# An encoder trunk on one core: the dense stream of the two merged stages is traced at 0.3 of attention's pace, where it was 1.1

## The chip, the core and the metric

The kernel runs on one core of a Trainium2 chip. The metric is the device time of one execution in microseconds (us), lower is better. Three runs of the kernel before gave 2283.27, 2291.74 and 2292.84 us, median 2291.74 us. The engines are named as the profile names them: PE (matrix multiply; PEld is its weight load), ACT (activations), DVE (vector), POOL (GpSimd) and SP (issues transfers).

## The reference

Two request groups share one set of weights: a prompt of 1024 tokens and a sample of 512, each with 16 learned meta tokens ahead. All is float32. One layer is computed:

```
n = rms_norm(h); qa,ka,va,qb,kb,vb = split(n @ w_in)          # 1024 -> 18 x 128 columns
A: 8 query heads, 2 key/value heads, per-head rms norm, axial rotary, softmax, @ va
B: 4 heads, two softmax maps each: (p0 - lam * p1) @ vb, then rms norm of the head
h = h + concat(A, B) @ w_out
n = rms_norm(h); gate = conv3(n @ w_ff_gate); h = h + (gelu(gate) * (n @ w_ff_up)) @ w_ff_down
y = rms_norm(h)                                                # D_FF = 2816 = 22 x 128
```

## The kernel before

The token axis is the free axis of every dense product. Each weight tile is 128 x 1024 float32 (512 KB). `load_weight` brings it in with a transfer issued from ACT's queue (L146), splits it into a high part (a cast: ACT on L123, or POOL on L150) and a low remainder (DVE, L124 or L151), and `mm3` (L129 to L131) multiplies three times: high by high, high by low, low by high. All weights of the program go through one pool `g.wp`: two raw slots `w_f` and three slots each of `w_hi` and `w_lo`. Slots are handed on in the order in which the tiles were traced, so a tile traced later can't get a slot before one traced earlier.

The program has these stages, all written as Python generators that yield the number of PE columns they have just traced:

1. `projection` of the sample, alone.
2. The first merge: `attention` of the sample with `projection` of the prompt; when attention is done, the rest of the projection is traced at once.
3. The second merge: `attention` of the prompt with the sample's dense stream `f1`, which is `mixer_out` (w_out) and then `conv_glu`: eleven pairs of feature tiles, each pair two gate tiles (chunks of 258 columns), two up tiles (512 columns) and two down tiles (512 columns; the last pair in 256).
4. The third merge: `mixer_out` of the prompt (chunks of 344, 342 and 340 columns, PSUM tag `s`) with what is left of `f1`, at 1.0 to 1.0; then the rest of `f1`, called a drain.
5. `conv_glu` of the prompt, alone. It takes its buffers where the sample's stood.

In attention, `softmax` fills three PSUM banks (`ps_s`, one buffer) with scores (PE, L401 and L402, 348 columns each), takes the row minimum of the negated scores on DVE (L405) and the exponential on ACT (L408). `weighted_v` transposes the probabilities on PE (L422, PSUM `ps_t`, two buffers), splits them (ACT L123, DVE L124, or `pt_hi`, `pt_lo`) and multiplies by v (A: L436, L437; B: L432 to L434; the tail L446) into `ps_o`, which has one buffer. A block of A is one head on 512 queries. The prompt has 16 of them, with a tile of 8 halo queries after each four heads. A differential block of B (L519 to L541) has three column tiles of 114 queries, each with two softmax maps: two exponentials, two scalings on ACT (L524, L527) and an addition on POOL (L528). It ends with a norm that also goes through `ps_o`: ACT copies `ps_o` (L533) and squares it (L535), PE sums (L537), ACT takes Ln, Exp and Square (L112 to L114), DVE two products (L115, L117) and the last product (L540). The prompt has twelve such blocks, after all of A.

What sets the order: `merge` calls whichever of the two generators is behind by its own scale, where `wa` and `wb` are the scales:

```
i = 0 if b is None or done[0] / wa <= done[1] / wb else 1
...
done[i] += next((a, b)[i])
```

It stops when `a` (attention) is done. From the traced order and the slots a scheduler then lays out each engine's instructions, and may put a later-traced instruction ahead of an earlier one where its slots and inputs allow it. At run time each engine runs its list in order.

Of the kernel before, what the change touches and what calls it, by code (L numbers as in the profile page):

```python
# [771 lines left out]
PADD = 8  # L772
ML = 2
NRAW, NW = 2, 3
R1, R2, R3 = (1.0, 1.1), (1.0, 1.1), (1.0, 1.0)


@with_exitstack
# [173 lines left out]
```

## Time and profile before

| what | value |
|---|---|
| median of three runs | 2291.74 us (2283.27 to 2292.84) |
| span of the profiled execution | 2286.9 us |
| median less that span | 4.8 us |
| PE busy | 2136.4 us, 93% of the span |
| DVE busy | 1273.1 us, 56% |
| ACT busy | 1032.2 us, 45% |
| POOL busy | 665.6 us, 29% |
| mean granted PE clock | 0.964 |

A matmul's busy time overlaps with the next one's, so a busy PE may run at very different paces; what a matmul costs in a stream is the distance between two starts. By the trace, the prompt's first scores start at 547.5 us, its last ones end at about 1370 us, its `mixer_out` starts at 1404.55 us and its `conv_glu` at 1524 us.

### The profile page before, as it was taken

Reading aid. Unit: us, or ns where it says so; the run is one execution under the profiler, and the core shown is the slowest. Engines: PE = TensorE matmul, PEld = TensorE weight load, DVE = VectorE, ACT = ScalarE, POOL = GpSimd, SP = SyncE. Lnnn points to the kernel's source line nnn. Section 1 sums busy time; section 2 is a strip of 40 time slices with the busy share of each in tenths; the row PEclk is TensorE's granted clock in tenths of the full one; section 3 lists DMA queues with packets and bytes.
Section 4 is the critical chain, followed back from the end, with each engine's and each line's share of the span. In section 5 each row is a group of like instructions: output and inputs, shape, how many; then the busy total and the mean of one; then the engine's idle time right before and its main releaser. Section 6 shows DMA issues by size and latency. Waiting matters only on the chain.

```text
span 2286.9 us, 32292 instructions
## 1 busy us (share of the span) xinstructions
PE 2136.4 (93%) x12418; PEld 1917.3 (84%) x12418; DVE 1273.1 (56%) x2203; ACT 1032.2 (45%) x1806; POOL 665.6 (29%) x514
## 2 busy tenths in 40 slices
PE   7888989997599999999999987989999999999997
PEld 6887888996488888888999975988888888888887
DVE  6635544455357666766777774774333444433445
ACT  5434544565346434456777785542122211122224
POOL 5862335442023212124444432431110001111004
PEclk9898999997799999999999997999999999999999
DMA  6564645444533332323333313631111111111112
GB/s 209 172 219 88 140 142 137 161 139 141 120 103 67 93 98 76 87 66 100 110 100 102 106 44 120 202 112 56 37 56 47 47 47 46 43 50 56 46 37 75
DMA packets 126739, 222.76 MB, mean 97 GB/s; under 512 B 28888, under 2 KB 79864, under 8 KB 126072
## 3 DMA queue, kind: packets, MB, share of 16 engines
q1 hardware_dynamic: 97784, 115.82, 17.4%
q10 hardware_dynamic: 28800, 104.87, 15.1%
q8 instruction: 98, 1.61, 0.3%
q14 instruction: 57, 0.47, 0.1%
HBM read 172.10 MB, written 48.55 MB: 96 GB/s over the span
## 4 chain that ended last, share of the span: by engine, by line
PE 67%; DMA 4%; DVE 4%; ACT 2%; issue 1%; SPq 0%; POOL 0%; POOLq 0%; DVEq 0%; ACTq 0%
PE ps_mm L129 17%; PE ps_mm L130 17%; PE ps_mm L131 17%; PE ps_t L422 4%; PE ps_s L401 3%; PE ps_s L402 3%; PE ps_o L437 1%; PE ps_o L436 1%; DMA res<-xT 1%; PE ps_o L432 1%; PE ps_o L434 1%; PE ps_o L433 1%; DMA v<-v 1%; DVE w_lo L124 1%; DMA rT<-r_a 1%
## 5 line engine op out<-in xcount | busy, mean ns | idle before, releaser
L129 PE MATMUL ps_mm<-xhi,w_hi 128*128 128x512 f32 (+6 forms) x1968 | 665.2, 338 | 29.5 <-ACT xhi L123 28.5
L130 PE MATMUL ps_mm<-xlo,w_hi 128*128 128x512 f32 (+6 forms) x1968 | 659.3, 335 | 0.0
L131 PE MATMUL ps_mm<-xhi,w_lo 128*128 128x512 f32 (+6 forms) x1968 | 657.4, 334 | 0.0
L129 PEld LDWEIGHTS ps_mm<-xhi,w_hi 128*128 128x128 f32 x1968 | 374.1, 190 | 54.4 <-ACT xhi L123 28.9
L130 PEld LDWEIGHTS ps_mm<-xlo,w_hi 128*128 128x128 f32 x1968 | 373.5, 190 | 25.0 <-issue 0.9
L131 PEld LDWEIGHTS ps_mm<-xhi,w_lo 128*128 128x128 f32 x1968 | 373.2, 190 | 24.1
L123 ACT CAST w_hi<-w_f 128x1024 fp32r<-128x1024 f32 x134 | 139.4, 1048 | 395.7 <-PE ps_mm L130 357.8
L405 DVE TENSOR_SCALAR_CACHE_REDUCE p<-ps_s 114x1044 f32<-114x1044 f32 (+5 forms) x212 | 223.4, 1054 | 130.3 <-PE ps_s L402 121.0
L124 POOL TENSOR_TENSOR a_lo<-gate,a_hi 128x512 fp32r<-128x512 f32 x66 | 100.3, 1520 | 658.1 <-ACT a_hi L123 654.2
L408 ACT ACTIVATE p<-p,nm 114x1040 f32<-114x1040 f32 (+5 forms) x212 | 215.2, 1015 | 89.3 <-DVE p L405 88.6
L123 ACT CAST pt_hi<-ps_t 128x512 fp32r<-128x512 f32 (+6 forms) x360 | 167.0, 484 | 193.1 <-PE ps_t L422 150.0
L699 DVE TENSOR_TENSOR h<-ps_mm,h 128x512 f32<-128x512 f32 (+1 forms) x288 | 182.1, 645 | 123.4 <-PE ps_mm L131 122.6
L124 DVE TENSOR_TENSOR pt_lo<-ps_t,pt_hi 128x512 fp32r<-128x512 f32 (+4 forms) x312 | 170.6, 563 | 118.0 <-ACT pt_hi L123 117.1
L130 PE MATMUL ps_mm<-a_lo,w_hi 128*128 128x512 f32 (+1 forms) x576 | 216.3, 379 | 0.0
L131 PE MATMUL ps_mm<-a_hi,w_lo 128*128 128x512 f32 (+1 forms) x576 | 215.7, 378 | 0.0
L129 PE MATMUL ps_mm<-a_hi,w_hi 128*128 128x512 f32 (+1 forms) x576 | 214.5, 384 | 0.0
L401 PE MATMUL ps_s<-k,q 128*114 128x348 f32 (+4 forms) x552 | 179.5, 331 | 21.5 <-DMA q<-qk 15.1
L422 PE MATMUL ps_t<-ident,p 128*128 128x128 f32 (+7 forms) x1188 | 187.6, 272 | 9.5 <-ACT p L408 6.2
L402 PE MATMUL ps_s<-k,q 128*114 128x348 f32 (+4 forms) x552 | 173.0, 319 | 10.9 <-DMA q<-qk 10.9
L422 PEld LDWEIGHTS ps_t<-ident,p 128*128 128x128 f32 (+7 forms) x1188 | 143.1, 137 | 41.8 <-issue 9.5
L124 DVE TENSOR_TENSOR w_lo<-w_f,w_hi 128x1024 fp32r<-128x1024 f32 x100 | 122.7, 1236 | 81.8 <-ACT w_hi L123 81.7
L687 DVE TENSOR_TENSOR gate<-ps_mm,gate 128x512 f32<-128x512 f32 x66 | 45.6, 691 | 198.3 <-PE ps_mm L131 195.7
(186 smaller groups left out, 3608.3 us busy)
## 6 DMA issues: line engine op xcount, KB each, us to landing
w_f<-w_gate ACTq DMA_DIRECT2D x44, 512.0 KB
w_f<-w_up ACTq DMA_DIRECT2D x44, 512.0 KB
w_f<-w_down ACTq DMA_DIRECT2D x44, 512.0 KB
w_f<-w_in ACTq DMA_DIRECT2D x36, 512.0 KB
w_f<-w_out ACTq DMA_DIRECT2D x32, 512.0 KB
q<-qk SPq DMA_DIRECT2D x48, 256.0 KB
q<-qk SPq DMA_DIRECT2D x48, 171.0 KB
qk<-hi SPq DMA_DIRECT2D x20, 384.0 KB
```

What stands on the lines that cost most here:

```text
L123: nc.scalar.copy(hi, src)
L124: (lo_engine or nc.vector).tensor_tensor(out=lo, in0=src, in1=hi.bitcast(F32), op=ALU.subtract)
L129: nc.tensor.matmul(ps, lhsT=whi, rhs=xhi, start=start, stop=False)
L130: nc.tensor.matmul(ps, lhsT=whi, rhs=xlo, start=False, stop=False)
L131: nc.tensor.matmul(ps, lhsT=wlo, rhs=xhi, start=False, stop=stop)
L401: nc.tensor.matmul(ps[:, i], lhsT=q[0], rhs=kc, start=True, stop=False)
L402: g.mark = nc.tensor.matmul(ps[:, i], lhsT=q[1], rhs=kc, start=False, stop=True).ins
L405: nc.vector.tensor_scalar(out=p.rearrange("p (i w) -> p i w", i=nch), in0=ps, scalar1=-HD ** -0.5, scalar2=3.0e38, op0=ALU.mult, op1=ALU.m ...
L408: nc.scalar.activation(p, p, AF.Exp, bias=nm, scale=-1.0, accum_out=l)
L422: nc.tensor.transpose(tps[:, c:c + M], p[:, k0:k0 + kw], g.ident[:M, :M])
L687: nc.vector.tensor_tensor(out=a, in0=up, in1=a, op=ALU.mult)
L699: nc.vector.tensor_tensor(out=hs, in0=ps, in1=hs, op=ALU.add)
```

## The change

One line of numbers changes. R1 holds the scales of the first merge (attention, then projection), R2 those of the second (attention, then `f1`), R3 those of the third.

```
-R1, R2, R3 = (1.0, 1.1), (1.0, 1.1), (1.0, 1.0)
+R1, R2, R3 = (1.0, 0.3), (1.0, 0.3), (1.0, 1.0)
```

Each instruction stays what it was; only places in the lists change. Up to a point that the run before reached at 615.7 us, PE's list is the same row for row, the whole first merge and the sample's attention included; the lists of ACT, DVE, POOL and SP also first differ in the second merge.

The first place is ACT's list in the second merge, behind the two weight loads of the down tiles that belong to the sample's second feature pair. Before, the next weight is a gate tile of the third pair:

```order
L408 ACTIVATE p,l_a<-p,nm 128x1040
L675 ACT_TABLE_LOAD
L675 ACTIVATE gate<-gate 128x1024
L678 ACT_TABLE_LOAD
L146 DMA w_f<-w_gate 128x1024
L458 COPY o_low<-ps_o 64x8
```

and now it is the first w_out tile of the prompt's `mixer_out`:

```order
L408 ACTIVATE p,l_a<-p,nm 128x1040
L675 ACT_TABLE_LOAD
L675 ACTIVATE gate<-gate 128x1024
L678 ACT_TABLE_LOAD
L146 DMA w_f<-w_out 128x1024
L123 CAST pt_hi<-ps_t 128x512
```

So the prompt's w_out tiles now stand in the weight slots from the end of the second pair on. The loads that follow in this list are one gate, two w_out, one gate and one w_out; then there is no weight load until the prompt's attention has ended.

The second place is PE's list in the eighth of the twelve differential blocks of the prompt, at the end of its product with v. Before, triples of the dense stream (`a_hi`, `a_lo`) stand between the pieces of attention:

```order
L432 MATMUL ps_o<-pt_hi,v 128x342
L433 MATMUL ps_o<-pt_hi,v 128x342
L434 MATMUL ps_o<-pt_lo,v 128x342
L422 MATMUL ps_t<-ident,p 128x114 x3
L129 MATMUL ps_mm<-a_hi,w_hi 128x256
L130 MATMUL ps_mm<-a_lo,w_hi 128x256
L131 MATMUL ps_mm<-a_hi,w_lo 128x256
L446 MATMUL ps_o<-pt_hi,v_tail 128x342
L422 MATMUL ps_t<-ident,p 128x114 x3
L401 MATMUL ps_s<-k,q 114x348
```

and now scores, transposes and products with v follow each other directly:

```order
L401 MATMUL ps_s<-k,q 114x348
L402 MATMUL ps_s<-k,q 114x348
L434 MATMUL ps_o<-pt_lo,v 128x342
L422 MATMUL ps_t<-ident,p 128x114 x3
L446 MATMUL ps_o<-pt_hi,v_tail 128x342
L422 MATMUL ps_t<-ident,p 128x114 x3
L401 MATMUL ps_s<-k,q 114x348
```

This holds from the last dense matmul of the second merge, which now stands ahead of the last 522 of the prompt's 828 score matmuls, to the end of attention.

The third place is PE's list where the sample's `f1` goes from an up tile (`xhi`, `w_lo`) to the down tiles (`a_hi`, `a_lo`) of a pair. Before, this stood in the second merge, and attention's instructions are near:

```order
L131 MATMUL ps_mm<-xhi,w_lo 128x512
L129 MATMUL ps_mm<-a_hi,w_hi 128x512
L130 MATMUL ps_mm<-a_lo,w_hi 128x512
L131 MATMUL ps_mm<-a_hi,w_lo 128x512
L402 MATMUL ps_s<-k,q 128x348
L401 MATMUL ps_s<-k,q 128x348
```

and now, for six of the pairs, it stands behind the prompt's `mixer_out`, with nothing but `f1` itself around it:

```order
L131 MATMUL ps_mm<-xhi,w_lo 128x512
L129 MATMUL ps_mm<-a_hi,w_hi 128x512
L130 MATMUL ps_mm<-a_lo,w_hi 128x512
L131 MATMUL ps_mm<-a_hi,w_lo 128x512
L129 MATMUL ps_mm<-a_hi,w_hi 128x512
L130 MATMUL ps_mm<-a_lo,w_hi 128x512
```

Counted over the lists between PE's first changed row and the prompt's `mixer_out`, the dense matmuls of `f1` before (1200 of 258 columns, 252 of 256, 1008 of 512) become 384, 168 and 192; so 816 of 258, 84 of 256 and 816 of 512 columns now stand behind attention, which is eight and a half of the eleven pairs.

## The prediction

> **What bounds the kernel now.** I first read the busy shares by slice.
>
> ```profile
> PE   7888989997599999999999987989999999999997
> PEclk9898999997799999999999997999999999999999
> ```
>
> PE is nearly full, with two dips: slices 10 and 11 (515 to 629 us, where the second merge begins) and slices 24, 25 and 27 (from 1315 us on, where the prompt's attention ends). Its granted clock is low there too (7 tenths). Then the busy time by stage, cut where PE's list first changes, at the last stretch of attention, at its end, and at the start of the prompt's `conv_glu`:
>
> ```profile
> core 0: us, PE busy (x) PEld busy (x) DVE busy (x) ACT busy (x) POOL busy (x), PEclk, DMA share, GB/s
> 615.70:700.00 84.30, 81.66 (x591) 74.73 (x590) 54.02 (x97) 44.11 (x86) 25.37 (x28) 1.00 0.39 99
> 700.00:1300.00 600.00, 598.91 (x3635) 530.25 (x3635) 429.35 (x714) 362.31 (x600) 191.02 (x155) 1.00 0.33 93
> 1300.00:1404.50 104.50, 87.26 (x516) 75.71 (x514) 68.06 (x126) 77.66 (x137) 31.79 (x23) 0.91 0.22 75
> 1404.50:1524.00 119.50, 106.46 (x600) 101.06 (x601) 87.31 (x131) 66.72 (x123) 55.85 (x47) 0.90 0.54 173
> ```
>
> From 700 to 1300 us PE is busy 598.91 of 600 us, while ACT has 362 and DVE 429: this stage is bound by PE, because dense matmuls fill every wait of attention. What a matmul costs here is the distance of starts (first column):
>
> ```profile
> 881.65 0.28 PE L130 MATMUL ps_mm<-xlo,w_hi 128*128 128x258 f32 x1
> 881.77 0.28 PE L131 MATMUL ps_mm<-xhi,w_lo 128*128 128x258 f32 x1
> ...
> 895.01 0.32 PE L401 MATMUL ps_s<-k,q 128*128 128x348 f32 x1
> 895.17 0.39 PE L437 MATMUL ps_o<-pt_lo,v 128*128 128x512 f32 x1
> 895.40 0.60 PE L422 MATMUL ps_t<-ident,p 128*128 128x128 f32 x4
> 895.75 0.47 PE L129 MATMUL ps_mm<-xhi,w_hi 128*128 128x512 f32 x1
> ...
> 896.30 0.40 PE L131 MATMUL ps_mm<-xhi,w_lo 128*128 128x512 f32 x1
> 896.53 0.39 PE L129 MATMUL ps_mm<-xhi,w_hi 128*128 128x512 f32 x1
> ```
>
> 258 columns cost 0.12 us, scores of 348 cost 0.16, 512 columns 0.23, four transposes 0.35. Dense work thus costs the same wherever it stands, if PE is fed. The question is how full PE is when attention stands alone. The trace shows that near its end, by L537, once per differential block:
>
> ```profile
> 1326.96 0.84 PE L537 MATMUL ps_o<-o_sq,ones_v 128*128 128x342 f32 x2 [0.91 <-ACT o_sq L535]
> ...
> 1351.03 0.74 PE L537 MATMUL ps_o<-o_sq,ones_v 128*128 128x342 f32 x2
> ...
> 1372.10 1.37 PE L537 MATMUL ps_o<-o_sq,ones_v 128*128 128x342 f32 x2
> ...
> 1404.55 0.66 PE L129 MATMUL ps_s<-xhi,w_hi 128*128 128x344 f32 x1 [1.52 <-ACT xhi L123]
> ```
>
> ```profile
> 1351.03:1372.10 21.07, 15.51 (x92) 12.54 (x91) 15.18 (x28) 18.45 (x34) 5.72 (x5) 0.99 0.03 10
> ...
> 557.00:574.70 17.70, 16.02 (x90) 12.78 (x90) 13.53 (x25) 13.38 (x25) 0.00 (x0) 1.00 0.36 82
> ```
>
> Between 1351.03 and 1372.10 no dense matmul runs: one block (its 92 PE instructions) takes **21.07 us with ACT busy 18.45**. By distances of starts the same 92 would need about 12 us: 31 scores and 25 products of 342 columns at 0.16, 33 transposes at 0.09. Alone, the differential block belongs to ACT and its chain, not to PE.
>
> **The change, part by part.** Stage 1 and the first merge cost nothing: no row moves before 615.7 us. There the rest of the projection is traced right behind attention, and the list comes out the same.
>
> In the second merge the stretch from 615.70 to 1404.55 us, 789 us, splits in two.
>
> *With dense work.* Up to the last dense matmul PE now has 228 score matmuls (36 us), 158 products of 512 (37), 336 transposes (30), the halo tile (4), and dense 384 + 168 of about 257 (66) and 192 of 512 (45): 218 us. The stretch 615.70 to 700 held 591 instructions in 84.3 us, or 0.143 each, the PE-full one 0.165; the 1494 rows of this part give 214 to 246 by these. I take **236**: 8% for switching and for a share of attention that is higher than before.
>
> *Attention alone.* Left are 92 products of 512, or 5.4 blocks of A, the second halo tile, and twelve differential blocks. For A:
>
> ```profile
> L405 DVE TENSOR_SCALAR_CACHE_REDUCE p<-ps_s 128x1044 f32<-128x1044 f32 x6 | 7.5, 1244 | 3.6 <-PE ps_s L402 3.5
> L124 DVE TENSOR_TENSOR pt_lo<-ps_t,pt_hi 128x512 fp32r<-128x512 f32 x7 | 4.5, 686 | 0.3 <-ACT pt_hi L123 0.3
> ```
>
> A block has four minima and nine splits: DVE 4 x 1.24 + 9 x 0.69 = 11.2 us, PE 3.8 + 3.2 + 4.0 = 11.0. The stretch 557 to 574.7, with six score tiles and hardly any dense work, took 17.7 us, or 11.8 per four. I take 13 (11 to 15): 70 us, and 5 for the halo. For B, ten periods of 21.1 bring L537 of the tenth block (211), and then 1404.55 - 1372.10 = 32.4 us end the last two, as before. Together **319 us** (A at 11 and B at 18.45, ACT's busy time: 281; A at 15 and B at 24.1, the distance from 1326.96 to 1351.03, which held some 9 us of dense work: 359).
>
> So the prompt's `mixer_out` starts 789 - 236 - 319 = **234 us sooner**.
>
> *What comes later.* Behind it stand 816 + 84 matmuls of about 257 columns at 0.12 and 816 of 512 at 0.234: 107 + 191 = **298 us**, at full pace. Their cover is gone too. From up to down tiles there is a chain:
>
> ```profile
> L687 DVE TENSOR_TENSOR gate<-ps_mm,gate 128x512 f32<-128x512 f32 x22 | 15.1, 688 | 29.0 <-PE ps_mm L131 26.4 <-ACT gate L675 2.5
> ...
> L123 ACT CAST a_hi<-gate 128x512 fp32r<-128x512 f32 x22 | 13.6, 618 | 14.4 <-DVE gate L687 14.3
> ...
> L124 POOL TENSOR_TENSOR a_lo<-gate,a_hi 128x512 fp32r<-128x512 f32 x22 | 32.8, 1489 | 43.1 <-ACT a_hi L123 39.3 <-issue 3.8
> ```
>
> 0.69 + 0.62 + 1.49 = 2.8 us, while the pair's first tile offers six matmuls on two PSUM buffers (1.4 us): some 1.4 us of wait in each of six pairs that stand alone, and a little for evictions into two buffers. I take **+10** (0 to 25).
>
> *The seams.* 1404.5 to 1524 us holds 576 w_out matmuls at 0.16 and little else, about 95 us in 119.5.
>
> ```profile
> 1522.33 1.50 PE L576 MATMUL ps_s<-acc,ones_d 128*128 128x340 f32 x2 [6.56 <-POOL acc L571]
> ```
>
> The 6.56 us at its end are now filled by `f1`; but `f1`'s own last norm and the prompt's eight first norm tiles then stand ahead of `conv_glu`, which I put at 13. Net **+6** (-10 to +15). The queues: ACT's list has no weight load while attention is alone, so no load waits there in front of exponentials; SP's loads of q come for shorter blocks, at a DMA share of 0.33 before.
>
> Sum: -234 + 298 + 10 + 6 = **+80 us**. The span of 2286.9 becomes 2367; the median lies 4.8 above that span, so **2372 us**.
>
> **Two rules.** After a long gap PE's pace falls:
>
> ```profile
> 1377.76 0.65 PE L432 MATMUL ps_o<-pt_hi,v 128*128 128x342 f32 x1 [4.30 <-DVE o_rs L115]
> 1378.21 0.49 PE L433 MATMUL ps_o<-pt_hi,v 128*128 128x342 f32 x1
> 1378.50 0.49 PE L434 MATMUL ps_o<-pt_lo,v 128*128 128x342 f32 x1
> ```
>
> After 4.30 us of waiting the distance is 0.29 us, where 348 columns had 0.16. [...] DVE is also held up by POOL's addition:
>
> ```profile
> 1356.20 2.41 POOL L528 TENSOR_TENSOR p<-p 114x1040 f32<-114x1040 f32 x1 [3.37 <-ACT p L527]
> ...
> 1357.14 1.85 DVE L117 SCALAR_TENSOR_TENSOR o_rs<-o_rs,rs_y 128x342 f32<-128x342 f32 x1
> ...
> 1391.80 0.52 DVE L117 SCALAR_TENSOR_TENSOR o_rs<-o_rs,rs_y 128x342 f32<-128x342 f32 x1
> ```
>
> 1.85 against 0.52 us, on the chain that frees `ps_o`. My 21.07 includes one such hit. [...]
>
> **The rivals.** *The clock falls while attention is alone* (12%). For: both dips of PE carry 7 tenths of clock. Against: 0.99 and 1.00 in the two stretches alone. At 0.29 for 0.16 PE's own work there, some 200 us at full pace (5.4 blocks at 11 and twelve at 12), needs 360 instead of the 319: 2372 + 41 = 2413 us.
>
> *Attention alone is tighter* (12%): blocks at ACT's busy time, no waits in `f1`: part two 281, +10 gone: 2324 us.
>
> *Not slower* (4%). The one mechanism: the differential blocks, freed of dense work, run at PE's 12.1 us instead of ACT's pace. Then ten of them take 121, and the whole comes out at 2372 - 90 = 2282 us. It decides at a period of 13.1 us, where ten blocks have won back the 80. Against it stand 18.45 us of ACT work in every block, which no order makes smaller.
>
> *Nothing moves* (1%): the scheduler could take dense work ahead as it does in the first merge. The lists show that it does not here: the weight slots are taken by w_out tiles, which wait for attention.
>
> **How the numbers follow.** My forecast, 2345 to 2400 us, has 71%. The range reaches to the tight rival's 2324 and beyond the clock's 2413, with waits at 25 and B at 24.1 partly together: 2324 to 2430. What a measurement can tell from no change is 0.5%, 11 us: slower 0.95, as all of the first three cases are (2324 is 1.4% above the median); the last two rivals hold 0.05, 0.03 of it within the 11 us (2282 is) and 0.02 below.
>
> **What would show it.** In the changed profile: PE's slices about 850 to 1170 us fall to 5 to 7 tenths with ACT at 8 or 9; L537 stands 20 to 23 us apart there; `mixer_out` of the prompt starts near 1170 us; `f1` alone follows at over 9 tenths, with waits of 1 to 2 us for `a_lo`; `conv_glu` starts near 1604. I am wrong if L537 is under 17 or over 25 us apart, if dense matmuls still stand there, or if `f1` alone shows waits for weights.

## The result, and the profile after

The changed kernel takes **2448.01 us** (median of four runs, 2446.67 to 2453.54), the kernel before in the same job 2290.18 us (2283.27 to 2292.84): ratio **1.0688**, 95% interval 1.0673 to 1.0703. Slower, as forecast, but by 158 us instead of 80, and above the upper end of the range (2430). The profiled execution has a span of 2446.6 us.

First the page's busy tenths per slice (a slice is now 61 us) in the changed kernel:

```profile
PE   7888999974999998777799999995999999999998
...
PEclk8989999987999998888899999997999999999999
```

The dip that stood at slices 24 to 27 (the end of attention) has become a wide one, slices 16 to 20 (918 to 1223 us), with a clock of 8 tenths, and a new narrow one stands at slice 28 (1651 to 1713 us). Then the windows, cut at the last dense matmul of the second merge, at the first and the tenth differential block (L537), at the prompt's `mixer_out` and at the sample's last norm:

```profile
core 0: us, PE busy (x) PEld busy (x) DVE busy (x) ACT busy (x) POOL busy (x), PEclk, DMA share, GB/s
615.70:859.60 243.90, 240.49 (x1558) 213.00 (x1558) 172.52 (x297) 137.19 (x250) 55.77 (x57) 1.00 0.42 91
859.60:975.90 116.30, 103.38 (x578) 84.31 (x576) 87.14 (x161) 95.00 (x165) 26.74 (x22) 0.94 0.23 61
975.90:1191.60 215.70, 156.59 (x802) 134.26 (x802) 137.90 (x243) 174.72 (x297) 72.76 (x55) 0.86 0.16 54
1191.60:1224.00 32.40, 22.40 (x103) 17.24 (x102) 12.51 (x25) 16.91 (x36) 2.58 (x2) 0.80 0.34 124
1224.00:1662.40 438.40, 407.11 (x2313) 357.42 (x2313) 227.04 (x313) 120.13 (x180) 119.89 (x107) 0.98 0.32 105
1662.40:2446.60 784.20, 754.11 (x3816) 659.71 (x3816) 341.86 (x510) 187.53 (x268) 106.00 (x88) 0.98 0.15 49
```

These rows can be set against the forecast's stretches. The third sum is 119.3 + 298 + 10 + 6, less the 1.5 us of the last norm's own row, at whose start (1522.33 before) both profiles are cut here; from there the kernel before had 2286.9 - 1522.3 = 764.6 us. The 13 us forecast for the seam into `conv_glu` are counted in the third sum, though most of the seam lies behind the cut.

| stretch | forecast | measured | difference |
|---|---|---|---|
| second merge with dense work | 236 | 243.9 | +8 |
| attention alone | 319 | 364.4 | +45 |
| `mixer_out`, rest of `f1` | 432 | 438.4 | +7 |
| from the last norm ahead of the prompt's `conv_glu` to the end | 765 | 784.2 | +20 |

So the plan of the stages was right and two terms were too small: **attention alone** and **the start of the prompt's `conv_glu`**. In the first, nine periods of L537 take 215.7 us, 24.0 each instead of 21.1 (26 of the 45), and A, the halo and the first differential block take 116.3 instead of 96 (20). The last two blocks take 32.4, as forecast.

How such a block looks is told by the timelines of PE, DVE and POOL (start, duration, what, and in brackets the wait ahead of it and its releaser):

```profile
1098.14 0.42 PE L401 MATMUL ps_s<-k,q 128*114 128x348 f32 x1 [1.14 <-DVE p L405]
...
1102.65 0.63 PE L401 MATMUL ps_s<-k,q 128*114 128x348 f32 x1 [3.29 <-DVE p L405]
1103.08 0.49 PE L402 MATMUL ps_s<-k,q 128*114 128x348 f32 x1
1103.37 0.49 PE L401 MATMUL ps_s<-k,q 128*114 128x348 f32 x1
```

```profile
1100.45 0.17 DVE L523 RECIPROCAL r_b<-l_b 114x2 f32<-114x2 f32 x1 [2.36 <-ACT p L408]
1101.34 1.25 DVE L405 TENSOR_SCALAR_CACHE_REDUCE p<-ps_s 114x1044 f32<-114x1044 f32 x1 [0.72 <-POOL p L528]
```

```profile
1098.91 2.39 POOL L528 TENSOR_TENSOR p<-p 114x1040 f32<-114x1040 f32 x1 [3.12 <-ACT p L527]
```

DVE stands at a reciprocal that waits for ACT's exponential, then at a minimum that waits for POOL's addition to end at 1101.30 (it frees a buffer of p). The next scores wait 3.29 us for that minimum, and then PE runs at 0.29 us per 348 columns instead of 0.16. Two suspects suggest themselves, the buffers of p and the lost clock; the experiments speak against both as the main cause. A third, the place of that reciprocal in DVE's list, no run moves by itself.

The second term shows in PE's and DVE's timelines at the seam:

```profile
1662.39 1.22 PE L576 MATMUL ps_mm<-acc,ones_d 128*128 128x256 f32 x2 [8.73 <-POOL acc L571]
1681.31 0.94 PE L129 MATMUL ps_mm<-xhi,w_hi 128*128 128x344 f32 x2 [17.70 <-ACT xhi L123]
```

```profile
1673.01 0.48 DVE L725 SCALAR_TENSOR_TENSOR y<-h,gain,rstd 128x256 f32<-128x256 f32 x1 [1.80 <-DMA yT<-y]
...
1680.81 0.58 DVE L646 SCALAR_TENSOR_TENSOR t<-h,gain,rstd 128x344 f32<-128x344 f32 x1 [3.98 <-DMA yT<-y]
```

PE waits 8.73 and 17.70 us. DVE's products of y (L725) wait for the stores of earlier y tiles, since the sample's y has two buffers, and the prompt's first norm tiles t (L646) stand behind them in DVE's list; one of these waits 3.98 us for a store itself. Before, `f1` ended long ahead of this point and all that was hidden.

### The profile page after: what moved, and what is told of

It reads as the page before. It is cut to its first block, busy times and chain, and to the rows that moved or that the text cites. A ratio compares the mean times of both kernels' runs of the same rounds, so it can differ in the third digit from the quotient of the medians.

```text
span 2446.6 us, 32351 instructions
## 1 busy us (share of the span) xinstructions
PE 2193.2 (90%) x12418; PEld 1940.3 (79%) x12418; DVE 1283.2 (52%) x2203; ACT 1033.8 (42%) x1806; POOL 651.5 (27%) x514
## 5 line engine op out<-in xcount | busy, mean ns | idle before, releaser
L401 PE MATMUL ps_s<-k,q 128*114 128x348 f32 (+4 forms) x552 | 192.0, 353 | 68.3 <-DVE p L405 53.1
L408 ACT ACTIVATE p<-p,nm 114x1040 f32<-114x1040 f32 (+5 forms) x212 | 215.1, 1015 | 52.6 <-DVE p L405 51.9
L402 PE MATMUL ps_s<-k,q 128*114 128x348 f32 (+4 forms) x552 | 180.2, 332 | 12.0 <-DMA q<-qk 12.0
L401 PEld LDWEIGHTS ps_s<-k,q 128*128 128x128 f32 (+3 forms) x552 | 107.1, 194 | 90.5 <-DVE p L405 72.8
L669 ACT ACTIVATE gate<-ps_mm,vec 128x256 f32<-128x256 f32 (+2 forms) x110 | 66.4, 606 | 265.0 <-PE ps_mm L131 249.1
```

The lines of the kernel that those rows point to most:

```text
L401: nc.tensor.matmul(ps[:, i], lhsT=q[0], rhs=kc, start=True, stop=False)
L402: g.mark = nc.tensor.matmul(ps[:, i], lhsT=q[1], rhs=kc, start=False, stop=True).ins
L408: nc.scalar.activation(p, p, AF.Exp, bias=nm, scale=-1.0, accum_out=l)
L669: nc.scalar.activation(a, gp[:, 1:cw + 1], AF.Identity, scale=cw3[1], bias=cb)
```

## The experiments

Each is the changed kernel with one edit, unless another is said. The numbers of a group were taken beside runs of the kernel before on the same chip (median 2282.22 us for e1 to e4, 2280.29 for e5 to e8, 2280.37 for e9 to e12, 2284.26 for e13 and e14), so they are compared by ratio. "Period" is the mean of nine distances of L537 (from the first to the tenth differential block; "fed" where dense matmuls stand between them), "alone" the stretch without dense matmuls that ends at the prompt's `mixer_out` (55 us in the kernel before).

| run | edit | ratio (95%) | alone, us | period, us |
|---|---|---|---|---|
| changed kernel | | 1.0688 (1.0673 to 1.0703) | 364 | 24.0 |
| e1 | rest of `f1` traced first | 0.9881 (0.9856 to 0.9905) | none | fed |
| e2 | ten p buffers | 1.0686 (1.0656 to 1.0716) | 358 | 24.7 |
| e3 | addition on DVE | 1.0675 (1.0648 to 1.0703) | 360 | 23.2 |
| e4 | eight y buffers | 1.0663 (1.0640 to 1.0687) | 364 | 24.0 |
| e5 | own slots for w_out | 1.0379 (1.0360 to 1.0398) | 41 | fed |
| e6 | p in groups | 1.0730 (1.0712 to 1.0747) | 366 | 24.8 |
| e7 | scaling and addition in one | 1.0486 (1.0465 to 1.0507) | 317 | 19.0 |
| e8 | ratio 0.6 | 1.0517 (1.0492 to 1.0541) | 249 | 25.1 |
| e9 | one PSUM buffer | one run, 2605.12 us | 300 | 23.5 |
| e10 | e9 with filling matmuls | one run, 2632.66 us | 325 | 24.7 |
| e11 | e1 with e7 | 0.9889 (0.9870 to 0.9907) | none | fed |
| e12 | e1 at ratio 1.0 | 1.0001 (0.9988 to 1.0014) | 32 | fed |
| e13 | one softmax less per block | one run, 2430.67 us | 357 | 23.5 |
| e14 | second scaling on DVE | one run, 2411.20 us | 344 | 22.7 |

### Is it the slots that keep the dense work out of attention?

e1 moves one line of the trace:

```
             merge(attention(es0, g, 0, "left"), R2[0], f1, R2[1])
         g.psum.relay(s=6)
+        drain(f1)
         st0 = state(ctx, 0, "left", False)
         merge(mixer_out(g, 0, st0, "left", False, "s"), R3[0], f1, R3[1])
```

> The changed kernel with one line moved: the rest of the sample's dense stream is traced right behind the prompt's attention, ahead of the prompt's mixer_out (so mixer_out has nothing beside it any more). The ratio stays 0.3. Theory (weight slots): it is the w_out tiles in the weight slots that kept the rest of the stream out of attention, not the ratio; with the slots free the scheduler lays the rest among the prompt's attention again, about 64 dense matmuls for 36 scores as before, and the time is 2275 to 2310 us. Rival 1 (the traced position itself): work traced behind attention comes last wherever it could go, and the time stays 2420 to 2450 us. Rival 2 (halfway): it goes back among attention but the loads of its weights make exponentials wait on the activation engine, 2310 to 2400 us.

Measured 0.9881, faster than the kernel before. Windows (columns as above) up to the prompt's first `mixer_out` matmul: of e1 from attention's last score on, of the kernel before from its last dense matmul of `f1` on:

```profile
1314.40:1369.20 54.80, 53.84 (x342) 48.14 (x341) 35.59 (x64) 28.23 (x55) 14.26 (x10) 1.00 0.45 154
```

```profile
1350.00:1404.50 54.50, 38.58 (x194) 30.50 (x192) 28.15 (x53) 36.50 (x70) 10.65 (x8) 0.83 0.22 79
```

In the kernel before, the last 54.5 us of attention have no dense work: 194 matmuls. In e1 the 54.8 us behind the last score hold 342 at full clock, 238 of them dense, so the end of attention is filled.

e5 leaves all order as it was and gives the w_out tiles slots of their own, opened ahead of the second merge:

```
+    w = (wp or g.wp).tile([P, D], F32, name="w_f", tag="w_f", bufs=1 if wp else NRAW)
...
-                w = load_weight(g, g.w_out[j])
+                w = load_weight(g, g.w_out[j], wp=g.wp2 if s == 0 else None)
```

> The changed kernel, everything traced in the same order and at the same 0.3, but the prompt's w_out tiles get a small weight pool of their own (one raw, one high, one low slot; paid for in the prompt's attention with three k buffers instead of four, two q instead of three, two pt instead of three). Theory (weight slots): with the shared slots free the rest of the sample's stream is laid among the prompt's attention although it is traced behind it, last scores come near 1310 to 1380 us, and the ratio to the kernel before is 0.99 to 1.03 (some of it paid for the narrower pools of attention). Rival (it is the ratio or the traced position, not the slots): the stretch without dense work stays and the ratio is 1.05 to 1.08.

The stretch alone went from 364 to 41 us, with the same tracing order and the same 0.3. The windows up to `mixer_out`:

```profile
545.00:1000.00 455.00, 424.71 (x2631) 373.15 (x2632) 302.74 (x515) 242.28 (x429) 97.36 (x90) 0.96 0.39 90
1000.00:1426.00 426.00, 388.66 (x2307) 345.56 (x2304) 274.76 (x480) 272.19 (x449) 158.36 (x117) 0.96 0.27 85
```

PE is 91 to 93% busy over all of attention. That the weight slots held the stream back is shown; that the ratio stayed at 1.038, above the 0.99 to 1.03 expected, goes with the narrower k, q and pt pools, or with the single w_out slot, which were not separated (its nine fed periods take 35.1 us in the mean, those of e1 30.5).

e12 puts 1.0 in place of 0.3 beside e1's edit. (Here and in e8 the first ratio is 1.1 again. PE's rows are the same with 1.1 and with 0.3 until the second merge is under way.)

> The second ratio at 1.0 with the rest of the sample's stream traced ahead of the prompt's mixer_out. In the lists 24 dense matmuls more than in the kernel before are left behind attention's last scores, where 0.3 with the same edit leaves 273. Theory (the 1.2% that this edit gained at 0.3 is the end of attention, which is fed there and stands alone in the kernel before): at 1.0 the end stands nearly alone again and the ratio is 0.994 to 1.003. Rival (the gain is the removal of the merge with mixer_out, or another thing that doesn't hang on the ratio): 0.985 to 0.991.

1.0001: by the trace 12 dense matmuls instead of 238 are left between attention's last score and `mixer_out`, and e1's gain is gone. So e1's 1.2% is the fed end of attention.

e8 is the dose, `R2 = (1.0, 0.6)`.

> The second ratio at 0.6 instead of 0.3 (the first one as before, which moves nothing). In the lists the dense work then ends ahead of the last 276 of the prompt's 828 scores (0.3: 522; 1.1: 24 matmuls are left beside the last 36 scores). Theory (the loss is the attention left alone, each differential block some 12 us over what its matmuls need when fed, plus a fixed part at the seams): 7.7 blocks alone, 3 of them also alone in the kernel before, so 55 to 70 us, and 20 to 30 us for waits in f1 and the seam into the prompt's conv_glu: ratio 1.030 to 1.045. Rival 1 (a fixed cost as soon as the stream is cut in two): ratio 1.055 or more. Rival 2 (a longer part of dense work with attention costs more than its matmuls, as the stretch with dense work did, 244 us against 236): ratio above 1.045 with the blocks alone at their 24 us.

1.0517, between theory and rival 1; rival 2 can't be told apart from it by this number. Put in a row, 55, 249 and 364 us alone give 1.000, 1.0517 and 1.0688: of 2290 us, the first 194 us more cost 118, the next 115 cost 39. What is left alone first is the end (differential blocks, which lose half their time), last the blocks of A (which lose less: 4.25 of them took the 64.2 us from 859.6 to 923.8 us, 15.1 each, where I had put PE's need at 11). So there is no fixed step. My expectation missed because it took 7.7 blocks alone, 3 of them alone before too: by the traces 318 scores stand behind e8's last dense matmul (8.8 blocks) and 36 in the kernel before (one). With the 7.8 blocks of difference its own sum gives 94 us and 20 to 30, where 118 were measured.

### What sets a differential block alone?

e2 adds a buffer of p, e6 keeps nine but divides them:

```
-    pp = pool(ctx, g, f"ap{s}", 9 if s == 0 else 6, side)
+    pp = pool(ctx, g, f"ap{s}", 10 if s == 0 else 6, side)
```

> The changed kernel with ten buffers for the prompt's probability tiles p where it had nine (paid for with two instead of three buffers for o_a and o_b and six instead of eight for the small tiles). Theory (slots of p): a differential block takes 24 us alone because the minimum of the next tile waits for the addition on GpSimd to free a slot, which makes a gap that halves TensorE's pace; with the tenth slot L537 stands 21 to 22.5 us apart, the half-pace stretch of the block goes, and the time is 2415 to 2432 us. Rival (the chain of the activation engine): the block's own 19 to 20 us of activations and their chain set the 24 us, L537 stays 23.5 to 24.5 us apart and the time 2440 to 2455 us.

```
+            p = pp.tile([P, ne], F32, name="p", tag="p", bufs=6)[:M]
+        else:
+            p = pp.tile([P, ne], F32, name="p", tag=f"p{own}", bufs=1)[:M]
```

(The calls choose the group; A's tiles are divided in the same way.)

> The changed kernel with the same nine buffers of p, but in three groups, so that the second map of a differential tile can't be given the slot that the addition before it has just released: six shared ones and one for the second map of each of the three tiles. The tenth slot of the run before it was no test of the slots, since the scheduler again handed out the one just released. Theory (the minimum that waits for the addition makes the gap that halves TensorE's pace): L537 stands 20.5 to 22.5 us apart (24.0 in the changed kernel), granted clock there 0.93 or more (0.86), ratio to the kernel before 1.052 to 1.062. Rival 1 (the activation engine's own chain sets the 24 us): period 23.5 or more, ratio 1.066 to 1.071. Rival 2: other waits take the place of this one, period 22.5 to 23.5, as with the addition on VectorE.

The waits in the nine periods in the changed kernel (who for whom, then us in all, times, longest):

```profile
PE ps_s L401 <- DVE p L405: 39.5, 30, 3.3
...
DVE p L405 <- POOL p L528: 7.5, 9, 1.2
```

and in e6, where the minimum stands on L408 and the scores on L404:

```profile
PE ps_s L404 <- DVE p L408: 43.5, 45, 1.4
DVE p L408 <- PE ps_s L405: 42.1, 46, 2.2
```

In e6 the wait for POOL is gone and no wait of PE for the minimum is over 1.4 us, yet the period is 24.8: the waiting has only been spread, and DVE's own wait for the scores has grown to 42.1 us, from 16.0. In e2 the wait stayed (7.1 us, ten times): the scheduler again handed out the buffer just released, so that run proves nothing about it. Taking this one wait away does not shorten a block; more than nine buffers that are really used were not tried. **The buffers of p are not shown to be the cause.**

e9 and e10 ask for the clock. e9 only changes the pools (`mm=1` and one bank `x`), e10 fills the gap with matmuls:

```
+            if s == 0:
+                with tc.issue_after(g.mark):
+                    d = g.psum.tile(P, 512, "x")
+                    for _ in range(8):
+                        nc.tensor.matmul(d, lhsT=qs[1][0][:, :P], rhs=ks[1][:, :512], start=True, stop=True)
```

> The control of the next run: the changed kernel with one PSUM buffer instead of two for the sample's dense stream beside the prompt's attention, the freed bank left unused. Only the steady distance of L537 and the granted clock there are read, not the total, which one buffer makes longer. Both theories: L537 23.5 to 24.5 us apart, clock 0.85 to 0.88, as in the changed kernel, since no dense work stands there.

> The control with eight matmuls of 512 columns (about 1.9 us, results used by nothing) behind the scores of the second map of each prompt's differential tile, into the free bank: TensorE does 5.6 us more per block, but the gap of 3.3 to 3.6 us in front of the next scores is closed to under 2 us. Theory C (the lost clock makes the difference between the 21 us that I took and the 24 measured): clock 0.95 or more and L537 20.5 to 22 us apart, although there is more work. Theory D (the 21 us came from a stretch with 30 of a block's 36 scores, so a whole block has one more softmax; the clock costs little, since TensorE waits anyway): the clock rises to 0.95 or more, but L537 stays 23 to 24.5 us apart.

Windows over the nine periods, e9 and then e10:

```profile
958.50:1170.20 211.70, 151.74 (x810) 127.51 (x808) 135.84 (x245) 178.11 (x303) 74.48 (x56) 0.90 0.17 56
```

```profile
976.40:1198.30 221.90, 182.95 (x1006) 154.16 (x1004) 118.58 (x238) 174.16 (x295) 68.78 (x55) 0.97 0.15 49
```

The clock rose from 0.90 to 0.97 and the period from 23.5 to 24.7. (The control's clock lies above the 0.85 to 0.88 expected, because two of its nine periods ran at full clock; e10's period lies a little above theory D's 24.5.) That speaks against the clock, with a reserve: the 5.6 us of added matmuls could have eaten a gain. In e7, e6 and e9, which add nothing to PE, periods with and without a half-pace stretch can be compared: in e7 18.7 us at a clock of 1.00 against 18.9 and 19.1 at 0.91; in e6 22.9 at 1.00 against 23.2 to 23.5 at 0.85; in e9 21.8 and 21.9 for the first and the fourth period at 1.00, where the changed kernel's same two took 22.6 at 0.85. The clock is worth 0.2 to 0.7 us of a block there, not three.

e13 leaves out one softmax per block (that tile's second map is taken from the one ahead), because the 21.07 us row of the kernel before had, counted in the trace, only 30 of a block's 36 scores:

```
+            few = s == 0 and len(pl) == 2
+            new = [softmax(...) for m in range(1 if few else 2)]
+            if few:
+                nc.vector.memset(l[:, 1:2], 1.0)
+                new.append(p1)
```

> The changed kernel without the second softmax (six scores, minimum, exponential) of the third tile of each prompt's differential block; that tile's second map is taken from the tile ahead of it, and its scalings and addition stay. A block then holds 30 scores, like the 21.07 us stretch of the kernel before from which I took a block's time. Theory D (that stretch was one softmax short of a block): L537 20.5 to 22 us apart where it was 24.0. Rival (the number of softmaxes doesn't set it, the chain behind them does): 23 to 24.5 us apart.

The period is 23.5, so the missing softmax was worth half a microsecond: this theory fell too. The changed kernel's own ninth period, which also has 30 scores, takes 23.5.

e3, e14 and e7 go at the work behind the exponentials: e3 moves the addition to DVE, e14 the second scaling, e7 does both in one DVE instruction:

```
-            nc.scalar.activation(p1, p1, AF.Copy, scale=c)
-            nc.gpsimd.tensor_tensor(out=p0, in0=p0, in1=p1, op=ALU.add)
+            nc.vector.scalar_tensor_tensor(out=p0, in0=p1, scalar=c, in1=p0, op0=ALU.mult, op1=ALU.add)
```

> The changed kernel with the addition of the two maps of a prompt's differential block on VectorE instead of GpSimd (L528, three per block; a third of its 2.4 us is also VectorE slowed down beside it). Theory (the addition is what holds the p slots and VectorE): the addition is over in 1.2 to 1.4 us, the minimum of the next tile no longer waits on it, L537 stands 21 to 23 us apart, and the time is 2415 to 2435 us. Rival (it is not the addition): VectorE has 4 us more per block on a chain that was set elsewhere, the period stays 24 to 25 us, and the time is 2445 to 2465 us.

> The changed kernel with the scaling of the second map on VectorE instead of the activation engine (three instructions per block, 3.4 us off the activation engine, 2 to 4 us more on VectorE); the addition stays on GpSimd. Theory A (the activation engine's work sets a block alone): L537 20 to 21.5 us apart. Rival (GpSimd's addition and what hangs on it set it; the fused run's gain came from there): 23 to 24.5 us apart.

> The changed kernel with the scaling of the second map and the addition of a prompt's differential tile in one VectorE instruction (L527 on the activation engine and L528 on GpSimd go, one scalar_tensor_tensor comes): per block the activation engine has 3.4 us less of its 19 to 20, GpSimd 7 us less, VectorE some 3.5 to 4 us more. Theory A (a block alone is bound by the activation engine and its chain): L537 20 to 21.5 us apart where it was 24.0, ratio to the kernel before 1.045 to 1.058. Theory B (bound by the alternation of scores and minimum through the one ps_s buffer and by VectorE): 22 to 24 us apart, ratio 1.06 to 1.07.

Windows over the nine periods, e3, e14 and e7:

```profile
968.20:1177.10 208.90, 156.14 (x807) 130.34 (x807) 153.14 (x271) 175.02 (x299) 5.31 (x28) 0.89 0.17 56
```

```profile
957.20:1161.60 204.40, 156.34 (x813) 128.68 (x811) 157.46 (x273) 151.27 (x275) 72.84 (x56) 0.91 0.18 58
```

```profile
961.20:1132.60 171.40, 142.41 (x810) 118.48 (x810) 151.76 (x271) 147.09 (x271) 5.14 (x27) 0.97 0.21 69
```

POOL's work off alone: 23.2. ACT's off alone (16.8 us per block instead of 19.4): 22.7. Both in one instruction: 19.0. e14 and e7 have about the same ACT work per block, and 22.7 against 19.0; so ACT's busy time alone does not set a block, which I had argued from one row. What only the fused form does is to take off both, and so to shorten the way from the exponentials to the transposes, from a scaling and an addition (1.15 and 2.4 us, on two engines) to one instruction of 1.30 us. That this shorter way is what gains the 5 us is argued: scaling and addition both on DVE, but as two instructions, were not run. PE's wait for the minimum then falls to

```profile
PE ps_s L401 <- DVE p L405: 8.0, 14, 1.5
```

from 39.5 us. DVE's wait at the reciprocal goes with it, from this in the changed kernel to this in e7:

```profile
DVE r_b L523 <- ACT p L408: 25.6, 18, 2.9
```

```profile
DVE r_b L523 <- ACT p L408: 1.6, 2, 1.0
```

Each edit lays DVE's list out anew. In the changed kernel the reciprocal stands ahead of the next tile's minimum and holds DVE up for 2.8 us per period; the 21.07 us row of the kernel before has no such wait. So the place of one small instruction is a rival that no run isolates. Against it stands e6, with no such wait and 24.8 us; e3 and e14 have 10.5 and 16.6 us of it. A block alone is a chain through four engines whose lists stand in a fixed order. Which link of it decides at which point was not separated further.

e11 puts the fusion on top of e1.

> Both edits that helped: the rest of the sample's stream traced ahead of the prompt's mixer_out (ratio 0.3) and the scaling and addition in one VectorE instruction. Theory (fed with dense work the attention is bound by TensorE, so activation work saved there is worth nothing, only the last blocks, alone again, gain 5 us each): 0.980 to 0.988 of the kernel before, against 0.988 without the fusion. Rival (VectorE's longer work delays the dense evictions): 0.989 to 0.995.

0.9889, inside e1's interval: the same instruction that is worth 5 us per block alone is worth nothing where dense work fills the waits. The last blocks did not give the small gain expected either; in e1 they are fed too.

### The seam

e4:

```
-                y = op.tile([P, ob, cw], F32, name="y", tag="y", bufs=2 if s == 1 else 4) if k % ob == 0 else y
+                y = op.tile([P, ob, cw], F32, name="y", tag="y", bufs=8 if s == 1 else 4) if k % ob == 0 else y
```

> The changed kernel with eight buffers for the sample's output tiles y where it had two. Theory (stores of y): the products of y on VectorE wait for y's stores, and the prompt's first norm tiles t stand behind them, so that TensorE waits 8.7 and 17.7 us at the start of the prompt's conv_glu; with eight buffers the two waits together are under 16 us and the time is 2432 to 2438 us. Rival (the norm chain itself): the waits stay within 3 us of 26 us and the time is 2445 to 2452 us.

PE's two waits in e4:

```profile
1656.32 1.22 PE L576 MATMUL ps_mm<-acc,ones_d 128*128 128x256 f32 x2 [10.60 <-POOL acc L571]
1666.49 0.94 PE L129 MATMUL ps_mm<-xhi,w_hi 128*128 128x344 f32 x2 [8.95 <-ACT xhi L123]
```

19.6 us instead of 26.4, between theory (under 16) and rival. The stores of y made half of the second wait. By e4's timeline the other half is mainly the norm's own chain behind the sample's last sums and the products of y, with 2.15 us of waiting for a store left; the first wait did not become shorter. By ratio e4 gains 0.25%, within the intervals of both.

## Why the prediction was right in direction and wrong in size

- **The first merge costs nothing**: right. The prompt's first score stands at 546.4 us, 547.5 before.
- **The dense work can't follow, because w_out tiles hold the slots**: right, and shown by e5 and e1. The rival that nothing moves was excluded for the right reason.
- **Second merge with dense work, 236**: 243.9, inside the bounds I gave from two rows (214 to 246). Half of the difference is a slip of counting: by the traces PE's first changed row stands at 622.3 us (623.8 in the changed kernel) and not at 615.7, and the 552 dense matmuls of about 257 columns were counted from there. From 615.7 us on the changed kernel has 587, or 35 x 0.12 = 4 us more.
- **Attention alone, 319**: this is the step that failed, by 45 us. The term "ten periods of 21.1" rested on one row of 21.07 us, read as a block at ACT's pace. Measured is 24.0, near the 24.1 that I had from the row beside it and had kept only as the upper end. The row was short of a softmax and came right out of the fed stretch, and the reason put on it, ACT's busy time, does not hold: e14 cuts that time by 2.6 us per block and the block only by 1.3. What the runs show in its place is that the scaling and the addition together cost a block alone 5 us (e7, 19.0), where taking off either of them leaves 23.2 or 22.7 (e3, e14); that they do so as a chain across engines is argued. Why the 21.07 us row was faster than the blocks of the changed kernel stays open. By the trace it held 30 of 36 scores and two of the three additions (POOL busy 5.72 us, 7.9 in a block of the changed kernel), and DVE never waited at the reciprocal, which it does for 2.8 us in a period of the changed kernel; e13 puts half a microsecond on the softmax.
- **A, the halo and the first differential block, 96**: 116.3. A took 15.1 us per block instead of 13, above my 15. From 923.8 to 956.5 us, where A gives way to the halo and B, PE's clock is 0.79 and half-pace rows stand from 941 to 953 us; some 9 us more than forecast went into the halo and the first differential block together.
- **Later dense work, 298 + 10 + 6 on top of `mixer_out`**: right to 7 us at the cut, with the 13 of the seam counted in. Without them 419 were forecast and 429.7 measured, up to PE's first wait at the seam; the difference lies within the 0 to 25 that I had allowed for waits.
- **The seam into `conv_glu`, 13**: the second mis-sized term. PE waits 26.4 us there, and from 1663 to 1700 us its clock is 0.70: 8.7 us of wait ahead of the cut and 19.6 us more behind it than before, 28 in all. I had counted the norm tiles but not the stores of y, which I had never looked at, because before nothing waited for them; e4 puts about 7 us on them.
- **The range**: it ended at 2430, below the sum of its own upper ends, 2372 + 10 + 40 + 15 + 9 = 2446 us (246 for 236, 359 for 319, 25 for 10, 15 for 6). Two terms went beyond theirs: attention alone by 5 us (364 for 359), and the seam by 6 (28, where +15 leaves room for 22).
- **DVE held up by POOL's addition**: the hit of the prediction's row comes back, but on another product. From 976 to 1130 us of the changed kernel L117 has a mean of 0.54 us; L540 takes 2.60 to 2.66 us once in each of eight of the nine periods, and 0.57 in the fourth. What in the addition holds DVE up, no run shows. The mean of L540 from 976 to 1130 us is, in the changed kernel and in e3, where POOL adds nothing beside it:

```profile
L540 DVE SCALAR_TENSOR_TENSOR o_b<-o_b,gsub,o_rs 128x342 f32<-128x342 f32 x7 | 16.3, 2323 | 0.2
```

```profile
L540 DVE SCALAR_TENSOR_TENSOR o_b<-o_b,gsub,o_rs 128x342 f32<-128x342 f32 x6 | 3.5, 576 | 0.2
```

  In e3 this product is 1.75 us shorter, but DVE also does three additions of 1.24 us per block, and the period gains 0.8 us.
- **The rival that the clock falls** (2413): the clock did fall, to 0.86, and yet it is a companion of the waits, not their price: with it held at 0.97 the block took no less (e10, 24.7 us, against 23.5 at 0.90 in e9), and where periods differ in the clock it is worth 0.2 to 0.7 us. (Of the slices 24, 25 and 27 that I had read as low in clock, only 25 shows 7 tenths.)

## What to carry to other kernels

A scheduler that may take later-traced work ahead can do so only if that work's buffers come free in time: when a shared pool hands slots out in traced order, one tile that waits for a late input closes the pool for all that follows, and the cheapest cure is to trace the work that can run first (e1, one line, 1.2% faster than the kernel before). Price a stage that loses its filler by several whole periods of it, not by the one that happens to be visible; count first whether that one holds a whole period's work. Don't put a busy time of 18 in 21 us down as a bound either: take away that work and see. And where a stage boundary moves, look at what was hidden at its end, stores and their buffers included.

## What the runs showed of the hardware that I had not expected

- The half pace starts after shorter pauses than the 4.30 us of the prediction's row, and not at one length. Over the sixteen traces, waits of PE of 2.25 to 3.0 us that began at full clock were followed by half clock within 1 us in 57 of 71 cases, waits of 3.0 to 3.5 us in 83 of 90, waits of 1.0 to 2.0 us in 106 of 487. In the traces of the kernel before and of the changed kernel alone these are 9 of 10, 9 of 9 and 8 of 45. (The same places come back from run to run, so these are fewer independent cases.)
- Beside POOL's addition a DVE product of 342 columns (L540) took 2.32 us in the mean from 976 to 1130 us of the changed kernel, 0.58 without it in e3: four times as long.
- Half pace, at which 348 columns took 0.29 us instead of 0.16, held for 15 to 22 matmuls of a block in the nine periods of the changed kernel. That is an estimated 2 to 3 us of PE time (0.13 us each), while periods with and without it (e6, e7, e9) lay 0.2 to 0.7 us apart: the waits of the block hid most of the slow PE.
